# Up projections of the second-type MLPs as seven quarter products, with weight sums built in DRAM on the way there

## The chip, the cores and the metric

The kernel runs on one core of one Trainium2 chip. The metric is device microseconds of that core. The core has a matmul engine (TensorE, PE in the profile, with PEld for its weight loads), a vector engine (VectorE, DVE), an activation engine (ScalarE, ACT), a general engine (GpSimd, POOL) and SyncE (SP), which here only issues transfers. PSUM, where matmuls add up, has eight banks of 128 x 512 float32.

## The reference, cut to what matters

A sequence of 512 tokens with 1024 channels goes through one first-type block and then twice through a second-type layer. The change lies in the second half of that layer:

```python
for l in range(2):
    h = rmsnorm(x, g_mix[l])
    x = x + mixer(h)          # latent attention and a 31-tap convolution
    h2 = rmsnorm(x, g_ffn[l])
    z = dwconv3(h2 @ w_up[l]) + b_dw_ffn[l]   # w_up: 1024 x 5632, three taps over the tokens
    zg, zv = split(z)                          # 2816 gates, 2816 values
    x = x + (silu(zg) * zv) @ w_down[l]        # 2816 x 1024
return rmsnorm(x, g_final)
```

## The kernel before, in words

Channels lie on partitions and tokens along the free axis. Every product is made with float32 split in two: a high part (`xh`, `whi`, a cast) and a low part (`xl`, `wlo`, what the cast left). `mm3` issues three matmuls for one block of 128 x 128 weights: high by high (L380), high weight by low input (L381), low weight by high input (L382), each over 512 tokens.

Weights come as **units** of eight such blocks, in the order of use that `weight_plan` writes down. `prep` loads a unit on SP's queue into one of three `raw` buffers (512 KB), casts it on ACT to `whi` (L359) and subtracts on POOL to get `wlo` (L360); `whi` and `wlo` have four buffers each. `take` calls `prep` for up to three units ahead of the one in use, so these instructions stand in ACT's and POOL's queues among the rest. All five queues run in order.

The MLP of a second-type layer has 22 pairs of a gate and a value projection, each 128 columns wide. `norm_in` splits the eight tiles of `x` and adds up their squares in `acc`; the norm's factor `r` isn't needed by the matmuls and is multiplied in afterwards (`conv3`, L1289). The first two pairs run side by side, one k-step of all four projections after another (`proj_outer`), while the norm's last tiles are still being made; then comes the total of `acc` (a matmul with ones, `total`) and from it `r`. The other pairs run one projection after another, 8 blocks each. For each pair: `b` times `r` on DVE, ACT starts a convolution tile (`cg` or `cv`, L1292), DVE adds two taps (L1293, L1294), ACT makes the silu, DVE multiplies gate and value (L1308), ACT and DVE split the product (`ah`, `al`). After 11 pairs (`CHUNK2`) come eight down projections over these 11 tiles, added to `x` (L1313), then the other 11 pairs. The last two down projections of all run as two halves of 256 tokens (`proj_halves`), and the final norm follows.

Of the kernel before, what the change touches and what calls it, by code (L numbers as in the profile page):

```python
# [21 lines left out]
P = 128  # L22
S = 512
# [22 lines left out]
NF2 = FF2 // P  # L46
CHUNK2 = 11
GLU_EARLY = 3
# [28 lines left out]
def _span(c0, n=P):  # L77
    return np.arange(c0, c0 + n)


def weight_plan():
# [47 lines left out]
    for l in range(NL):  # L129
# [29 lines left out]
        for i in range(NYB, KT):  # L159
            add(tiles("w_o_2", l, k8, _span(P * i)))  # L160
        for c in range(NF2 // CHUNK2):
            fs = list(range(c * CHUNK2, (c + 1) * CHUNK2))
            if c == 0:
                add(outer("w_up_2", l, KT, [_span(P * f + o) for f in fs[:2] for o in (0, FF2)]))
                fs = fs[2:]
            for f in fs:
                add(tiles("w_up_2", l, k8, _span(P * f)))
                add(tiles("w_up_2", l, k8, _span(FF2 + P * f)))
            add([("w_down_2", l, P * k, _span(P * m)) for m in range(KT) for k in range(c * CHUNK2, (c + 1) * CHUNK2)])
    return units  # L170


def pack_weights(inputs, plan):
    out = np.zeros((len(plan), P, UNIT * P), np.float32)
    for u, blocks in enumerate(plan):
        for b, (name, l, r0, cols) in enumerate(blocks):
            w = inputs[name] if l is None else inputs[name][l]
# [4 lines left out]
    return out  # L182


# [69 lines left out]
class Kern:  # L254
    def __init__(self, tc, xT, w, vec, cst, pos, outT):
        self.tc, self.nc = tc, tc.nc
        self.xT, self.w, self.vec_d, self.cst_d, self.pos_d, self.outT = xT, w, vec, cst, pos, outT
        self.plan = weight_plan()
        self.units = {}
        self.prepped = 0  # L260
        self.cur, self.blk = 0, 0
        self.table, self.table_users = None, []


    def setup(self, ctx):
# [22 lines left out]
        self.epst = c.tile([P, 1], F32, name="epst")  # L288
        nc.gpsimd.memset(self.epst, EPS)
        self.lna = {}  # L290
        for n in (D, 512, QL, KVL):
# [58 lines left out]
    def prep(self, u, eng=None):  # L350
        nc = self.nc
        n = len(self.plan[u]) * P
        raw = self.wp.tile([P, UNIT * P], F32, name="raw", bufs=3)
        hi = self.wp.tile([P, UNIT * P], FR, name="whi")
        lo = self.wp.tile([P, UNIT * P], FR, name="wlo")
        cuts = (0, n) if eng is None else (0, n // 2, n)
        for cs in map(slice, cuts, cuts[1:]):
            nc.sync.dma_start(out=raw[:, cs], in_=self.w[u, :, cs])
            nc.scalar.copy(out=hi[:, cs], in_=raw[:, cs])  # L359
            (eng or nc.gpsimd).tensor_tensor(out=lo[:, cs], in0=raw[:, cs], in1=hi[:, cs].bitcast(F32), op=ALU.subtract)  # L360
        self.units[u] = (hi, lo)

    def take(self, n=1, ahead=AHEAD):
# [38 lines left out]
    def proj_outer(self, pool, tag, acts, n, parts=WHOLE, between=None):  # L402
# [90 lines left out]
    def norm_in(self, pool, gname, l, on_pool=KT - 2):  # L493
# [13 lines left out]

        def finish(pp, tag):
            r = self.rp.tile([P, S], F32, name="r", bufs=1)
            self.rsqrt(r, self.total(pp, tag, acc)[0], D)  # L510
            return r

# [469 lines left out]
    def layer2(self, l, carry=None):  # L982
# [301 lines left out]
        split_in()  # L1284
        ffc = tc.tile_pool(name="ffc", bufs=CHUNK2, reuse_waits="tile")
        fp = ffc.__enter__()

        def conv3(ps, f, tag):
            V.tensor_tensor(out=ps, in0=ps, in1=r, op=ALU.mult)  # L1289
            w3 = self.v("w_dw_ffn_2", l, 3 * f, 3)  # L1290
            c = fp.tile([P, S], F32, name=tag, bufs=2)
# [4 lines left out]

        for c in range(NF2 // CHUNK2):
            a = []
            pss = []
            if c == 0:  # L1300
                pss = self.proj_outer(pp, "b", acts, 4)
                r = fin(pp, "b")
            for f in range(c * CHUNK2, (c + 1) * CHUNK2):
                pg, pv = pss[2 * f : 2 * f + 2] if 2 * f < len(pss) else (self.proj(pp, "b", acts), self.proj(pp, "b", acts))
                cg = conv3(pg, f, "cg")
                cv = conv3(pv, NF2 + f, "cv")
                self.act(AF.Silu, out=cg, in_=cg)
                V.tensor_tensor(out=cg, in0=cg, in1=cv, op=ALU.mult)  # L1308
                a.append(self.split(fp, cg, ("ah", "al")))
            tail = 2 if l == NL - 1 and c == NF2 // CHUNK2 - 1 else 0  # L1310
            for m in range(KT - tail):
                ps = self.proj(pp, "b", a)
                V.tensor_tensor(out=self.x[m], in0=self.x[m], in1=ps, op=ALU.add)  # L1313
            if tail:
                self.final(pp, a)
        self._close(ffc)
        self._close(xg)
        self._close(pp_)

    def final(self, pp, a):  # L1320
# [16 lines left out]
        def half(j, ps, cs):  # L1337
            i = KT - 2 + j
            V.tensor_tensor(out=self.x[i][:, cs], in0=self.x[i][:, cs], in1=ps, op=ALU.add)
            gain(i, cs, cs.start == 0 or j == 0)  # L1340

        def norm(cs):
            self.rsqrt(r[:, cs], self.total(pp, "b", acc[:, cs], *late)[0], D)
            late.clear()
            for j in range(0, KT, OUT_TILES):
                o = op.tile([P, OUT_TILES, S // 2], F32, name="o")
                for i in range(OUT_TILES):
                    (G if j + i in OUT_POOL else V).tensor_tensor(out=o[:, i, :], in0=self.x[j + i][:, cs], in1=r[:, cs], op=ALU.mult)
                dst = self.outT[j * P : (j + OUT_TILES) * P, cs].rearrange("(i p) s -> p i s", p=P)
                (nc.sync if j // OUT_TILES % 2 else nc.scalar).dma_start(out=dst, in_=o)  # L1350
# [40 lines left out]
```

## Time and profile before

| | |
|---|---|
| median of 3 runs | 1880.58 us (1879.61 to 1883.46) |
| the profiled execution's own time | 1880.29 us |
| its span, first to last instruction | 1878.6 us |
| granted TensorE clock, mean | 0.998 |
| TensorE busy | 1839.2 us, 98% |
| DVE, ACT, POOL busy | 958.1, 946.3, 938.4 us |
| MLP of layer 0 and of layer 1 | about 924 to 1310 us and 1506 to 1867 us |

A row of the timeline gives start and duration in us, engine, line, operation and output<-input; where several alike follow each other it gives their count behind an x, and the time that they cover together. A row of the groups gives line, engine, operation, names and shapes, count, then busy us in all, mean ns of one, and the idle time ahead of them. A row of the windows gives the stretch, its length, then for PE, PEld, DVE, ACT and POOL busy us with the count of instructions, then the granted clock (1 is full speed), the share of the DMA engines that is busy, and GB/s. Matmuls overlap in the pipeline, so what one costs is read from start to start, not from its duration.

### The profile page before, as it was taken

How to read it: one execution, taken by the hardware profiler on the slowest of the kernel's cores; microseconds unless marked ns; L12 is line 12 of the kernel's file. 1: busy time of each engine (PE TensorE's matmuls, PEld its weight loads, DVE VectorE, ACT ScalarE, POOL GpSimd, SP SyncE). 2: the span in 40 equal slices, each digit the busy share in tenths (PEclk: the TensorE clock that was granted, in tenths of full speed). 3: DMA queues.
4: the chain of work that ended last, by engine and by line, in shares of the span. 5: the costliest groups of instructions: out<-in, count | busy, mean ns of one | idle time of the engine just before them, and what ended most of it. 6: DMA issues, size and time to landing. Idle time of an engine off the chain costs nothing.

```text
span 1878.6 us, 22097 instructions
## 1 busy us (share of the span) xinstructions
PE 1839.2 (98%) x8448; PEld 1495.8 (80%) x8448; DVE 958.1 (51%) x1420; ACT 946.3 (50%) x1442; POOL 938.4 (50%) x510
## 2 busy tenths in 40 slices
PE   8999999999999999999999999999999999999997
PEld 6877888888888888766888888888866788888886
DVE  4666552724022037997565225522898565405543
ACT  6766633643243347697554224433778554314442
POOL 5233444644444557866644444454966464444442
PEclk9999999999999999999999999999999999999999
DMA  5111223222222222200222222222210122222221
GB/s 188 68 57 62 79 101 135 93 94 101 92 99 98 94 90 71 98 29 21 94 106 95 97 101 91 101 101 90 91 51 23 64 99 101 101 91 101 100 91 56
DMA packets 48649, 164.89 MB, mean 88 GB/s; under 512 B 5536, under 2 KB 7584, under 8 KB 48544
## 3 DMA queue, kind: packets, MB, share of 16 engines
q1 hardware_dynamic: 46304, 160.34, 24.3%
q10 hardware_dynamic: 2240, 3.15, 0.5%
q8 instruction: 66, 1.08, 0.2%
q14 instruction: 39, 0.32, 0.1%
HBM read 161.37 MB, written 2.10 MB: 87 GB/s over the span
## 4 chain that ended last, share of the span: by engine, by line
PE 89%; DVE 6%; ACT 3%; issue 1%; POOL 1%; DMA 0%; SPq 0%; DVEq 0%; ACTq 0%; POOLq 0%
PE b L381 23%; PE b L382 23%; PE b L380 23%; PE mm L381 3%; PE s L1140 3%; PE mm L380 3%; PE mm L382 3%; PE t L1157 2%; DVE xl L452 1%; PE av L1162 1%; PE av L1163 1%; PE cv L480 1%; ACT whi L359 1%; DVE x L650 1%; PE b L480 1%
## 5 line engine op out<-in xcount | busy, mean ns | idle before, releaser
L360 POOL TENSOR_TENSOR wlo<-raw,whi 128x1024 fp32r<-128x1024 f32 x300 | 720.9, 2405 | 809.9 <-ACT whi L359 809.6
L359 ACT CAST whi<-raw 128x1024 fp32r<-128x1024 f32 (+1 forms) x302 | 313.6, 1040 | 506.4 <-PE b L381 414.6
L380 PE MATMUL b<-xh,whi 128*128 128x512 f32 (+1 forms) x1296 | 495.4, 382 | 2.7 <-ACT xh L451 2.7
L381 PE MATMUL b<-xl,whi 128*128 128x512 f32 (+1 forms) x1296 | 491.4, 379 | 3.4 <-DVE xl L452 3.4
L382 PE MATMUL b<-xh,wlo 128*128 128x512 f32 (+1 forms) x1296 | 491.1, 379 | 0.0
L381 PEld LDWEIGHTS b<-xl,whi 128*128 128x128 f32 x1296 | 244.1, 188 | 51.9 <-DVE xl L452 4.2
L380 PEld LDWEIGHTS b<-xh,whi 128*128 128x128 f32 x1296 | 244.2, 188 | 50.5 <-ACT xh L451 3.1
L382 PEld LDWEIGHTS b<-xh,wlo 128*128 128x128 f32 x1296 | 244.1, 188 | 45.6
L380 PE MATMUL b<-ah,whi 128*128 128x512 f32 (+1 forms) x646 | 243.6, 377 | 0.0
L381 PE MATMUL b<-al,whi 128*128 128x512 f32 (+1 forms) x646 | 243.2, 377 | 0.0
L382 PE MATMUL b<-ah,wlo 128*128 128x512 f32 (+1 forms) x646 | 243.2, 376 | 0.0
L381 PEld LDWEIGHTS b<-al,whi 128*128 128x128 f32 x646 | 121.6, 188 | 22.4
L380 PEld LDWEIGHTS b<-ah,whi 128*128 128x128 f32 x646 | 121.5, 188 | 22.4
L382 PEld LDWEIGHTS b<-ah,wlo 128*128 128x128 f32 x646 | 121.6, 188 | 22.0
L1228 POOL TENSOR_TENSOR cacc<-cacc,pd 128x510 f32<-128x510 f32 (+14 forms) x94 | 119.8, 1275 | 26.6 <-ACT pd L1226 22.8
L1212 DVE SCALAR_TENSOR_TENSOR cv<-u,vec,cv 128x497 f32<-128x497 f32 (+13 forms) x146 | 108.2, 741 | 8.4 <-ACT cv L1202 6.5
L1289 DVE TENSOR_TENSOR b<-b,r 128x512 f32<-128x512 f32 x88 | 61.0, 697 | 97.3 <-PE b L382 97.1
L1313 DVE TENSOR_TENSOR x<-x,b 128x512 f32<-128x512 f32 x30 | 20.6, 687 | 161.3 <-PE b L382 161.3
L448 ACT CAST ah<-cg 128x512 fp32r<-128x512 f32 x44 | 27.3, 621 | 98.7 <-DVE cg L1308 98.7
L380 PE MATMUL mm<-xh,whi 128*128 128x512 f32 x176 | 69.3, 394 | 0.0
L871 DVE TENSOR_TENSOR b<-rl,b 128x512 f32<-128x512 f32 x32 | 22.1, 696 | 92.5 <-ACT rl L870 92.5
L381 PE MATMUL mm<-xl,whi 128*128 128x512 f32 x176 | 68.7, 391 | 0.0
(430 smaller groups left out, 2851.0 us busy)
## 6 DMA issues: line engine op xcount, KB each, us to landing
raw<-w SPq DMA_DIRECT2D x295, 512.0 KB, 3.2
x<-xT SPq DMA_DIRECT2D x8, 256.0 KB, 6.5
x<-xT ACTq DMA_DIRECT2D x8, 256.0 KB, 4.8
raw<-w SPq DMA_DIRECT2D x7, 256.0 KB, 2.6
outT<-o ACTq DMA_DIRECT2D x4, 256.0 KB, 2.4
outT<-o SPq DMA_DIRECT2D x4, 256.0 KB, 2.5
vec<-vec SPq DMA_DIRECT2D x1, 363.0 KB, 6.9
f<-pos SPq DMA_DIRECT2D x1, 256.0 KB, 3.3
```

The source lines that it names most:

```text
L359: nc.scalar.copy(out=hi[:, cs], in_=raw[:, cs])
L360: (eng or nc.gpsimd).tensor_tensor(out=lo[:, cs], in0=raw[:, cs], in1=hi[:, cs].bitcast(F32), op=ALU.subtract)
L380: mm(ps, lhsT=wb[0], rhs=xb[0], start=start, stop=False, **kw)
L381: mm(ps, lhsT=wb[0], rhs=xb[1], start=False, stop=False, **kw)
L382: mm(ps, lhsT=wb[1], rhs=xb[0], start=False, stop=stop, **kw)
L448: nc.scalar.copy(out=hi, in_=src)
L480: self.nc.tensor.matmul(full[:, :n], lhsT=self.ones, rhs=a, start=i == 0, stop=i == len(parts) - 1)
L1140: mm(s, lhsT=q[:, qb * P : (qb + 1) * P], rhs=k, start=True, stop=True)
L1157: nc.tensor.transpose(pt[:, qb * P : (qb + 1) * P], probs[qb][:, t * P : (t + 1) * P], self.ident)
L1212: ins = V.scalar_tensor_tensor(out=acc[:, o], in0=us[i][:, u], scalar=self.v("w_dw_conv_2", l, i * CONV_K + k), in1=acc[:, o], op0=ALU.mul ...
L1228: G.tensor_tensor(out=acc[:, o], in0=acc[:, o], in1=pd, op=ALU.add)
L1289: V.tensor_tensor(out=ps, in0=ps, in1=r, op=ALU.mult)
```

## The change

In both layers pairs 0 to 3 stay as they were, and pairs 4 to 21 use a scheme of seven products (Strassen and Winograd's). A pair's weights are four quarters: `a11`, `a12` (gate, the first and the last four k-blocks), `a21`, `a22` (value). The inputs are four quarters too: k-blocks 0 to 3 or 4 to 7, tokens 0 to 255 or 256 to 511. Seven products of a weight quarter or sum (`S1` to `S4`) and an input quarter or sum (`B11`, `B21`, `T1` to `T4`, `B22`), with three copies (`snap`) and three additions (`plus`) between, give both projections. So a pair takes 7 x 4 x 3 = 84 matmuls of 256 columns in place of 2 x 8 x 3 = 48 of 512, and 28 blocks of weights in place of 16.

- **Input sums.** `quarter_inputs` multiplies `r` into `x` ahead of the products and makes the seven input matrices with their splits: per layer 27 instructions on DVE, 14 casts on ACT, 6 subtractions on POOL. The value comes out negated, which tap weights of the other sign (`wneg`, made at the start) take back; the multiplication by `r` falls away for these pairs. For that, `total` and `r` are made after three of the eight k-steps of `proj_outer` in place of after all.
- **Weight sums.** The quarters come in a new input `wq`. `S1` to `S4` of all pairs are built in DRAM while the kernel runs: 40 copies on ACT's queue and 40 adding transfers on POOL's queue, most of 1 MB (groups of four pairs) and some of 0.5 MB, each issued behind the cast or the subtraction of a unit in `SIDE`: every unit from 10 to 48, every second to 111, then every one, which reaches to about unit 121. Unit 29 to 48 is the end of block 1's mixer, 49 to 112 its MLP, 113 to 140 the mixer of layer 0.
- **Order.** Chunks are 7, 7 and 8 pairs in place of 11 and 11, so the additions to `x` are 24 per layer in place of 16. Each product pair's last two products come among the next pair's, at a chunk's end among the first three down projections. 355 units are loaded in place of 302; units of the new kind that hold parts of two matrices take two loads.
- **End.** Output tiles of the last four channel blocks of the left half are issued behind the right half's last addition to `x`.

```diff
-CHUNK2 = 11
+CHUNKS2 = (0, 7, 14, 22)
+PLAIN2 = 4
+OUTER2 = 2
+NDOWN = 3
+SUM_PAIRS = 4
+SIDE = {u: 1 for u in range(10, 140) if u < 49 or u > 112 or u % 2}
...
         self.units[u] = (hi, lo)
+        for _ in range(SIDE.get(u, 0)):
+            if self.side:
+                begin, on_pool = self.side.popleft()
+                self.issue_behind(begin(), rest if on_pool else cast)
...
+        def copy(dst, src):
+            return lambda: nc.scalar.dma_start(out=dst, in_=src)
+        def add(dst, src):
+            return lambda: nc.gpsimd.dma_start(out=dst, in_=src, accum_op=ALU.add, max_dma_last_dim=row)
...
             for k, a in enumerate(acts):
+                if k == OUTER_LAG + 2 and between is not None:
+                    between()
                 for ps in pss:
...
+        def norms():
+            rs.append(fin(pp, "b", True))
+            self.quarter_inputs(hp, ops, "g_ffn_2", l, rs[0][1])
+        pss = self.proj_outer(pp, "b", acts, 2 * OUTER2, between=norms)
+        pss += [self.proj(pp, "b", acts) for _ in range(2 * (PLAIN2 - OUTER2))]
...
+                    for ps in (pg, pv):
+                        V.tensor_tensor(out=ps, in0=ps, in1=r, op=ALU.mult)
+                    a.append(unit(f, pg, pv, self.v("w_dw_ffn_2", l, 3 * (NF2 + f), 3), False))
...
+                def p4(g):
+                    times(g["v"][:, L], "T4", False, True)
+                    plus(g["v"][:, R], g["g"][:, R], g["u3"])
+                def p3(g):
+                    times(g["g"][:, R], "B22", False, True)
+                    plus(g["g"][:, R], g["g"][:, R], g["u2"])
+                    a.append(unit(g["f"], g["g"], g["v"], self.wneg[l][:, 3 * g["f"] : 3 * g["f"] + 3]))
...
+                    times(g["v"][:, L], "B11", True, False)
+                    u1 = snap(g["v"][:, L])
+                    times(g["g"][:, L], "B21", True, True)
+                    plus(g["g"][:, L], g["g"][:, L], u1)
+                    if old is not None:
+                        p4(old)
+                    times(g["v"][:, L], "T2", False, False)
+                    g["u2"] = snap(g["v"][:, L])
+                    times(g["g"][:, R], "T1", False, False)
+                    if old is not None:
+                        p3(old)
+                    times(g["v"][:, L], "T3", False, False)
+                    g["u3"] = snap(g["v"][:, L])
+                    old = g
...
+        for k in range(0, KT // 2, 2):
...
+                    V.scalar_tensor_tensor(out=t[:, j], in0=self.x[k0 + j], scalar=self.v(gname, l, k0 + j), in1=r, op0=ALU.mult, op1=ALU.mult)
...
+            def put(name, src, eng):
+                hi, lo = (t[:, k : k + 2] for t in ops[name])
+                A.copy(out=hi, in_=src)
+                eng.tensor_tensor(out=lo, in0=src, in1=hi.bitcast(F32), op=ALU.subtract)
...
+            put("B11", b11, G)
+            put("B21", b21, G)
+            t1 = temp()
+            V.tensor_tensor(out=t1, in0=b11, in1=b12, op=ALU.subtract)
...
+            put("T2", t2, V)
+            put("T1", t1, V)
...
+                    if behind is not None and j >= KT // 2 and not on_pool:
+                        self.issue_behind(ins, behind)
```

**How the order moves.** DVE, behind the norm's factor of layer 0, in the kernel before: `b_7868` to `b_7871` are the four projections of pairs 0 and 1 (gate, value, gate, value), and the convolution of pair 0 follows three multiplications by `r`.

```order
L491 SCALAR_TENSOR_TENSOR r_7992<-b_7993,r_7992 128x512 [waits DVE_49]
L1289 TENSOR_TENSOR b_7868<-b_7868,r_7992 128x512 [waits DVE_49,PE_49]
L1289 TENSOR_TENSOR b_7869<-b_7869,r_7992 128x512 [waits PE_49]
L1289 TENSOR_TENSOR b_7870<-b_7870,r_7992 128x512 [waits PE_49]
L1293 SCALAR_TENSOR_TENSOR cg_8002<-b_7868,vec_67,cg_8002 128x511 [waits Activation_49]
L1293 SCALAR_TENSOR_TENSOR cv_8007<-b_7869,vec_67,cv_8007 128x511 [waits Activation_49]
L1294 SCALAR_TENSOR_TENSOR cg_8002<-b_7868,vec_67,cg_8002 128x511 [waits DVE_49]
L1294 SCALAR_TENSOR_TENSOR cv_8007<-b_7869,vec_67,cv_8007 128x511 [waits DVE_49]
L1293 SCALAR_TENSOR_TENSOR cg_8019<-b_7870,vec_67,cg_8019 128x511 [waits Activation_49]
L1308 TENSOR_TENSOR cg_8002<-cg_8002,cv_8007 128x512 [waits DVE_49,Activation_49]
```

DVE at the same place in the changed kernel: `b_8011` to `b_8014` are pairs 0 and 1, `b_8199` to `b_8294` the four plain projections behind them, `T4l` the last input sum.

```order
L1448 TENSOR_TENSOR b_8014<-b_8014,r_8063 128x512 [waits PE_49]
L1540 TENSOR_TENSOR T4l_8005<-t_8112,T4h_8004 128x512 [waits Activation_49]
L1448 TENSOR_TENSOR b_8199<-b_8199,r_8063 128x512 [waits PE_49]
L1448 TENSOR_TENSOR b_8230<-b_8230,r_8063 128x512 [waits PE_49]
L1448 TENSOR_TENSOR b_8262<-b_8262,r_8063 128x512 [waits PE_49]
L1448 TENSOR_TENSOR b_8294<-b_8294,r_8063 128x512 [waits PE_49]
L1425 SCALAR_TENSOR_TENSOR cg_8335<-b_8011,vec_67,cg_8335 128x511 [waits Activation_49]
L1425 SCALAR_TENSOR_TENSOR cv_8339<-b_8012,vec_67,cv_8339 128x511 [waits Activation_49]
L1426 SCALAR_TENSOR_TENSOR cg_8335<-b_8011,vec_67,cg_8335 128x511 [waits DVE_49]
L1426 SCALAR_TENSOR_TENSOR cv_8339<-b_8012,vec_67,cv_8339 128x511 [waits DVE_49]
L1425 SCALAR_TENSOR_TENSOR cg_8352<-b_8013,vec_67,cg_8352 128x511 [waits Activation_49]
L1435 TENSOR_TENSOR cg_8335<-cg_8335,cv_8339 128x512 [waits DVE_49,Activation_49]
```

All eight multiplications now stand ahead of the first convolution step, the last of them behind the end of the last plain projection.

ACT in the changed kernel, the same stretch: `whi_8401` is the fourth unit of the first products, in the buffer that the last plain projection used.

```order
L406 CAST whi_8296<-raw_8295 128x1024 [waits DMAHW6_49,DMAHW7_49,PE_49,Pool_49]
L406 CAST whi_8401<-raw_8400 128x1024 [waits DMAHW0_49,DMAHW1_49,PE_49,Pool_49]
L1424 ACTIVATE cg_8335<-b_8011,vec_67 128x512
L1424 ACTIVATE cv_8339<-b_8012,vec_67 128x512
L1424 ACTIVATE cg_8352<-b_8013,vec_67 128x512 [waits DVE_49,PE_49]
L1424 ACTIVATE cv_8356<-b_8014,vec_67 128x512 [waits DVE_49]
L385 ACTIVATE cg_8335<-cg_8335 128x512 [waits DVE_49,Activation_49]
L561 CAST ah_8346<-cg_8335 128x512 [waits DVE_49]
L1424 ACTIVATE cv_8372<-b_8230,vec_67 128x512 [waits Activation_49]
L1454 COPY snap_8419<-b_8398 128x256 [waits PE_49]
```

The first convolution step `cg_8335` stands behind that cast, and the first `snap` behind silu and split of pair 0.

TensorE in the changed kernel, from the last plain projection to the first product: `b_8398` is the accumulator of the first product, in the bank of `b_8011`.

```order
L493 MATMUL b_8294<-xh_7949,wlo_8202 128x512
L491 MATMUL b_8294<-xh_7951,whi_8201 128x512
L492 MATMUL b_8294<-xl_7952,whi_8201 128x512
L493 MATMUL b_8294<-xh_7951,wlo_8202 128x512
L491 MATMUL b_8398<-B11h_7994,whi_8232 128x256 [waits DVE_49,Activation_49]
L492 MATMUL b_8398<-B11l_7995,whi_8232 128x256
```

The first product waits for DVE's last reading of pair 0's gate, the second tap `cg_8335<-b_8011` (L1426).

POOL in the changed kernel, block 1: the first adding transfers (512 rows of 2 KB) among the subtractions.

```order
L452 DMA S1_0_0_138<-wq 512x512 [waits DMAHW1_49]
L407 TENSOR_TENSOR wlo_1411<-raw_1409,whi_1410 128x1024 [waits DMAHW2_49,PE_49,Activation_49]
L407 TENSOR_TENSOR wlo_1525<-raw_1523,whi_1524 128x1024 [waits DMAHW4_49,PE_49,Activation_49]
L452 DMA S1_0_1_142<-wq 512x512
L407 TENSOR_TENSOR wlo_1565<-raw_1563,whi_1564 128x1024 [waits DMAHW5_49,PE_49,Activation_49]
...
L452 DMA S1_0_2_146<-wq 512x512
```

POOL had the subtractions alone there; an adding transfer now stands behind every second unit.

## Rows read from the trace of the kernel before

**Rows 1.** Page, part 1: busy time of TensorE.

```profile
PE 1839.2 (98%) x8448; PEld 1495.8 (80%) x8448; DVE 958.1 (51%) x1420; ACT 946.3 (50%) x1442; POOL 938.4 (50%) x510
```

**Rows 2.** Windows, MLP of layer 0 and of layer 1: busy time per engine.

```profile
945.00:1100.00 155.00, 155.00 (x683) 127.97 (x683) 70.34 (x98) 61.65 (x76) 67.37 (x29) 1.00 0.28 98
...
1527.00:1700.00 173.00, 173.00 (x763) 142.86 (x763) 75.09 (x105) 66.79 (x82) 76.23 (x32) 1.00 0.28 97
```

**Rows 3.** Timeline of TensorE, start of layer 0's MLP: start, duration.

```profile
923.73 0.39 PE L380 MATMUL b<-xh,whi 128*128 128x512 f32 x1
923.96 0.39 PE L381 MATMUL b<-xl,whi 128*128 128x512 f32 x1
```

**Rows 4.** Timeline of TensorE in the last down projections, 256 columns.

```profile
1862.04 0.28 PE L381 MATMUL b<-al,whi 128*128 128x256 f32 x1
1862.16 0.28 PE L382 MATMUL b<-ah,wlo 128*128 128x256 f32 x1
```

**Rows 5.** Timeline of the weight loads beside them.

```profile
1862.05 0.19 PEld L382 LDWEIGHTS b<-ah,wlo 128*128 128x128 f32 x1
```

**Rows 6.** Groups by line and shape, 945 to 1100 us (POOL, ACT, DVE).

```profile
L360 POOL TENSOR_TENSOR wlo<-raw,whi 128x1024 fp32r<-128x1024 f32 x29 | 69.6, 2401 | 89.1 <-ACT whi L359 89.1
...
L359 ACT CAST whi<-raw 128x1024 fp32r<-128x1024 f32 x29 | 30.5, 1052 | 58.1 <-PE b L381 58.0
L1292 ACT ACTIVATE cg<-b,vec 128x512 f32<-128x512 f32 x11 | 8.5, 772 | 3.3 <-DVE b L1289 3.3
...
L344 ACT ACTIVATE cg<-cg 128x512 f32<-128x512 f32 x11 | 6.9, 631 | 12.2 <-DVE cg L1294 12.2
L448 ACT CAST ah<-cg 128x512 fp32r<-128x512 f32 x11 | 6.8, 621 | 23.1 <-DVE cg L1308 23.1
...
L1289 DVE TENSOR_TENSOR b<-b,r 128x512 f32<-128x512 f32 x22 | 15.1, 695 | 16.7 <-PE b L382 16.6
...
L1294 DVE SCALAR_TENSOR_TENSOR cg<-b,vec,cg 128x511 f32<-128x511 f32 x11 | 8.2, 746 | 0.2
```

**Rows 7.** Page, part 6: weight loads, time from issue to landing.

```profile
raw<-w SPq DMA_DIRECT2D x295, 512.0 KB, 3.2
```

**Rows 8.** Groups by line and shape, whole span: 128x256 steps of DVE and ACT.

```profile
L534 DVE TENSOR_TENSOR x<-x,b 128x256 f32<-128x256 f32 x32 | 13.3, 416 | 0.7
...
L462 ACT ACTIVATE sq<-x 128x256 f32<-128x256 f32 x31 | 12.6, 407 | 8.9 <-DVE x L1339 6.6 <-POOL acc L463 2.0
```

**Rows 9.** Timeline of DVE and POOL, norm ahead of layer 0's MLP.

```profile
919.43 9.67 DVE L452 SCALAR_TENSOR_TENSOR xl<-x,vec,xh 128x512 fp32r<-128x512 f32 x5
...
932.00 0.68 DVE L463 TENSOR_TENSOR acc<-acc,sq 128x512 f32<-128x512 f32 x1
...
920.60 2.86 POOL L360 TENSOR_TENSOR wlo<-raw,whi 128x1024 fp32r<-128x1024 f32 x1
```

**Rows 10.** Timeline of DVE, the norm's factor of layer 0's MLP made.

```profile
949.50 0.69 DVE L491 SCALAR_TENSOR_TENSOR r<-b,r 128x512 f32<-128x512 f32 x1
```

**Rows 11.** Timeline of DVE and POOL, first pair of layer 1.

```profile
1537.38 1.73 DVE L1308 TENSOR_TENSOR cg<-cg,cv 128x512 f32<-128x512 f32 x1
...
1536.16 2.41 POOL L360 TENSOR_TENSOR wlo<-raw,whi 128x1024 fp32r<-128x1024 f32 x1 [5.12 <-ACT whi L359]
```

**Rows 12.** Timeline and windows of TensorE, end of block 1: idle, then clock.

```profile
696.03 0.38 PE L380 MATMUL b<-xh,whi 128*128 128x256 f32 x1 [2.32 <-ACT xh L451]
697.45 0.39 PE L381 MATMUL b<-xl,whi 128*128 128x256 f32 x1 [1.03 <-DVE xl L452]
...
699.00:703.00 4.00, 4.00 (x21) 3.64 (x20) 3.90 (x11) 2.72 (x7) 2.40 (x3) 0.62 0.18 68
```

**Rows 13.** DMA rate in 40 slices, and ACT's issues, 290 to 330 us.

```profile
GB/s 0 279 246 0 213 311 123 348 270 279 373 408 268 45 33 274 217 0 0 139 373 12 0 106 377 41 0 0 4 266 254 0 0 0 164 356 4 0 0 29
...
296.20 3.09 ACTq L314 DMA_DIRECT2D x<-xT  x6
```

**Rows 14.** Waits of TensorE from 1864 us to the end.

```profile
PE b L480 <- DVE acc L463: 0.5, 1, 0.5
```

More of the change, by code (lines that the diff above doesn't have):

```diff
@@ L78, in _span, with chunks2 @@
     return np.arange(c0, c0 + n)
+def chunks2():
+    return [range(a, b) for a, b in zip(CHUNKS2, CHUNKS2[1:])]
 def weight_plan():
@@ L160, in weight_plan @@
             add(tiles("w_o_2", l, k8, _span(P * i)))
[L161 to L169, printed above, removed]
+        ffn = [("w_up_2", l, P * k, _span(P * f + o)) for k in range(KT) for f in range(OUTER2) for o in (0, FF2)]
+        ffn += [("w_up_2", l, P * k, _span(P * f + o)) for f in range(OUTER2, PLAIN2) for o in (0, FF2) for k in range(KT)]
+        for ks in chunks2():
+            quarter = lambda which, f: [(which, l, f, kk) for kk in range(KT // 2)]
+            before = None
+            for f in ks:
+                if f >= PLAIN2:
+                    ffn += quarter("a11", f) + quarter("a12", f)
+                    if before is not None:
+                        ffn += quarter("a22", before)
+                    ffn += quarter("S2", f) + quarter("S1", f)
+                    if before is not None:
+                        ffn += quarter("S4", before)
+                    ffn += quarter("S3", f)
+                    before = f
+            down = [("w_down_2", l, P * k, _span(P * m)) for k in ks for m in range(NDOWN)]
+            ffn += down[:4] + quarter("a22", before) + down[4:8] + quarter("S4", before) + down[8:]
+            ffn += [("w_down_2", l, P * k, _span(P * m)) for m in range(NDOWN, KT) for k in ks]
+        add(ffn)
     return units
@@ L289, in setup @@
         nc.gpsimd.memset(self.epst, EPS)
+        self.wneg = {}
+        for l in range(NL):
+            t = c.tile([P, 3 * NF2], F32, name=f"wneg{l}")
+            nc.gpsimd.tensor_scalar(out=t, in0=self.v("w_dw_ffn_2", l, 3 * NF2, 3 * NF2), scalar1=-1.0, scalar2=None, op0=ALU.mult)
+            self.wneg[l] = t
         self.lna = {}
@@ L355, in prep @@
         lo = self.wp.tile([P, UNIT * P], FR, name="wlo")
[L356 to L360, printed above, removed]
-        self.units[u] = (hi, lo)
+        if eng is None and any(b[0] in QUARTERS + SUMS for b in self.plan[u]):
+            for c0, c1, src in self.sources(u):
+                nc.sync.dma_start(out=raw[:, c0:c1], in_=src)
+            cuts = ((0, n),)
+        else:
+            cuts = ((0, n),) if eng is None else ((0, n // 2), (n // 2, n))
+            for c0, c1 in cuts:
+                nc.sync.dma_start(out=raw[:, c0:c1], in_=self.w[u, :, c0:c1])
@@ L1295, in conv3, with unit @@
             return c
[L1297 to L1315, printed above, removed]
+        def unit(f, pg, pv, wv, in_psum=True):
+            cg = conv3(pg, self.v("w_dw_ffn_2", l, 3 * f, 3), f, "cg")
+            cv = conv3(pv, wv, NF2 + f, "cv")
+            to = pg if in_psum else cg
+            self.act(AF.Silu, out=to, in_=cg)
+            V.tensor_tensor(out=to, in0=to, in1=cv, op=ALU.mult)
+            return self.split(fp, to, ("ah", "al"))
```

173 lines of the change are left out of this document (160 added, 13 removed).

## The prediction

> **What bounds the kernel now.** I read the busy times first. TensorE is busy for 1839.2 of 1878.6 us [rows 1]; the profiled execution took 1880.29 us, 1.7 us more than its span, and lies 0.3 us under the median, so I work from 1880.3 us. The windows then tell whether that holds where the change is made: in both layers' MLPs TensorE is busy for the whole stretch at full clock, while DVE, ACT and POOL are at 39% to 45% and the DMA engines at 28% [rows 2]. There the time is the number of matmuls by their spacing, and only what changes these two, or makes TensorE wait, can move the end. All other engines have room before, so the question is whether they still have it after.
>
> **The change part by part: matmuls.** The spacing is read from start to start: 0.227 us for 512 columns, from 923.73 to 923.96 [rows 3] (24 matmuls of a unit take 5.44 us), and 0.120 us for 256 columns [rows 4]. A plain pair takes 48 x 0.2267 = 10.88 us, a product pair 84 x 0.120 = 10.08 us. One pair saves 0.80 us, 36 pairs 28.9 us. The eighth fewer multiplications would be 1.36 us a pair, 49 us in all, if 256 columns took half of 512; 13 ns more for each short matmul takes 20 us of that.
>
> Each of those short matmuls had a weight load of its own, and these follow each other in 0.12 us too although one lasts 0.19 us [rows 5], so the loads overlap with the matmuls and I take 0.120. The Trainium skill speaks against that: TensorE: Matmul & The Clock Gate, "The mechanism", lets a weight load overlap with matmuls in flight only if it goes to another group of rows of the array, and its section on LDWEIGHTS gives 107 ns for 128 columns. With its 109 and 216 ns for matmuls a pair would then go from 48 x 0.323 = 15.5 to 84 x 0.216 = 18.1 us, some 94 us slower in all, near 1997 us with the waits below. The trace has neither spacing.
>
> **Start of each MLP.** Taken per layer, with layer 0 as the example.
>
> The total now stands after three k-steps. The outer product starts at 923.73 [rows 3]; 36 matmuls are through at 931.9. DVE's last addition to `acc` starts at 932.00 and takes 0.68 us [rows 9], so TensorE waits until 932.7 and a little for the signal: 0.9 us. Before, the total came 13 us later and waited for nothing.
>
> The first product waits for a PSUM bank: that of pair 0's gate, until DVE has read it for the second tap. In DVE's order that step stands behind the multiplication of the last plain projection, and in ACT's order the convolution stands behind a cast that waits for the same projection's end. From that end the chain is cast 1.05, `cg` 0.77, first tap of the gate 0.75, first tap of the value 0.75, second tap of the gate 0.75 [rows 6], 4.1 us in all. Before, pair 0's steps ran while TensorE did the next pairs and waited for nothing [rows 2]. Above this floor, `quarter_inputs` may still be in DVE's way: 27 instructions that cost 0.7 us alone (19 us), 16 of them with two SBUF inputs. Such ones took 1.93 us each beside POOL's subtractions and additions (5 in 9.67 us, [rows 9]) and 1.73 us once beside a `wlo` [rows 11]. `r` was done 4.7 us behind the outer product's end, at 950.2 [rows 10], and will be at about 938 now; TensorE gets to the first product at 969 (192 matmuls of 512 from 923.73, the wait of 0.9, as much for the total). In these 31 us eight multiplications of 0.70 us [rows 6] are due too, so at 1.0 us each DVE's work is 27 + 5.6 = 33 us, a little late. A walk through the queues with stretched durations gives 5.4 us of wait, which I take, between 4.1 and 8.
>
> The first `snap` stands on ACT behind pair 0's silu and split. From the bank's release: second tap of the value 0.75, first tap of pair 1's gate 0.75, product of gate and value 0.7 to 1.7, `ah` 0.62, a `cv` 0.77, `snap` 0.41 [rows 6, 8, 11], 4.0 to 5.0 us; TensorE has two products of 1.44 us to do meanwhile and waits 1.1 to 2.1 for the third. I take 1.8, and 1.7 more for the rest: four plain pairs leave DVE some 17 us of taps and splits that run into the first product pairs, whose `plus` steps release products. Together 3.5 us, between 1.1 and 6.
>
> A wait of that length can cost clock. At the end of block 1 came waits of 2.3 and 1.0 us with one matmul between, and the clock from 699 to 703 was 0.62 of full speed [rows 12], that is 1.5 us lost. Part of such a loss lies under other waits: 1.2 us, between 0 and 1.7.
>
> Sum per layer 0.9 + 5.4 + 3.5 + 1.2 = 11.0 us, for two 22 us (bounds 12 and 33).
>
> **Steady product pairs.** A pair of 10.08 us needs 3.5 units, one in 2.88 us, where a unit lasted 5.44 us. POOL: 3.5 x 2.40 = 8.4 us. ACT: 3.5 x 1.05, three `snap` of 0.41, two starts of 0.77, silu 0.63, `ah` 0.62: 7.7 us. DVE: three `plus` of 0.42, four taps of 0.75, two of 0.7: 5.7 us [rows 6, 8]. Transfers: 1.84 MB, 182 GB/s, while the slices show up to 408 GB/s [rows 13]. None is over 85%. A `raw` buffer's round is issue 0.4, landing 2.85, cast 1.05, subtraction 2.4 [rows 6, 7], with queueing some 7.2 us for three buffers: 2.4 us a unit, 0.5 under the need. I cost it at nothing; without that cover see below. The two products that close a chunk leave 6.8 us for a chain of about 6 us (`plus`, tap steps, silu, product, split) before the last block of `down` needs them: 0 to 1 us, six times; I take 1 us.
>
> **Weight sums.** 75 MB are written under block 1 and the start of layer 0's mixer. The DMA engines are at 28% there as elsewhere, and a load's landing (3.2 us, [rows 7]) is far under the distance to its use of more than 5.4 us a unit. An issue on ACT's queue costs 0.5 us (six in 3.09, [rows 13]), 40 of them beside casts of 1.05 us that have a unit's 5.44 us. No row shows what an adding transfer costs POOL: nothing at best, and 2.6 us at 1 MB by 408 GB/s if POOL is held for all of it; with a `wlo` that makes 5.0 of the 5.44 us of a unit. I take 0, between 0 and 5 us. By the Trainium skill, DMA: Bandwidth & Descriptors, such a transfer takes 2.0 us and its bytes by 436 GB/s, 4.4 us here by estimate, and no run here shows it.
>
> **End.** The right half's total waits 0.5 us for `acc` [rows 14], behind output multiplications that now come later: 0.5 us gained.
>
> Sum: 1880.3 - 28.9 + 22 + 1 + 0 - 0.5 = 1874 us. With all bounds low 1863, all high 1896.
>
> **Rivals.**
> - **The start is covered.** If DVE gets to the convolution at the floor of 4.1 us, the products behind don't wait and the clock holds, a layer costs 0.9 + 4.1 = 5.0 us: 1880.3 - 28.9 + 10 - 0.5 = 1861 us. For it: DVE is at 45% [rows 2], the two-input steps are 0.7 us when alone. Against it: the queues are in order and the rows of the order put `snap` behind pair 0.
> - **Weights come too late (slower).** POOL at 83% and ACT at 76% both work on each unit in turn, and `wlo` took up to 2.86 us beside DVE [rows 9]. The two MLPs use 126 units in product pairs. From 2.94 us a unit on (0.06 x 126 = 7 us) the gain that I forecast is gone. A round of the three buffers of 9 us, which is 1.8 us of queueing over the 7.2, makes 3.0 us a unit, 15 us lost: 1889 us. Against it: four buffers of `whi` and `wlo` even out single delays, and only an average counts.
> - **Adding transfers hold POOL.** In the mixers POOL has convolution work too and a transfer can't hide there as in an MLP. Five of them at 2.6 us bare make 13 us: 1887 us.
> - **The short matmuls don't gain.** At 10.88 / 84 = 0.1295 us a matmul the products save nothing, and the start's waits stay: 1903 us. Against it [rows 4, 5]. The rule on weight loads would go far beyond; the trace leaves it next to no chance.
>
> **How the numbers follow.** 0.45 for the forecast (its own range 1868 to 1880), 0.27 for a covered start (1852 to 1867), 0.15 for late weights (1882 to 1900), 0.08 for POOL held, 0.05 for matmuls without gain. About 0.2%, 3.8 us, is what a measurement tells from no change. Faster than 1876.8: 0.30 of the first, all of the second, 0.03 of the others, 0.60. Within: 0.14 of the first, 0.04 of the others, 0.18. Slower: 0.22. The range 1857 to 1889 leaves out a quarter of the covered start, half of the late weights and the last case, under 0.2.
>
> **What would show it.** In the profile after: 256-column matmuls 0.120 us apart in the product pairs, 10.1 us a pair, or TensorE's waits there name `whi` or `wlo` (late weights); the first product of a layer waiting 4 to 8 us, released by DVE's second tap, and then `snap`; a granted clock under 1 behind it; no new waits of TensorE before about 924 us, or POOL late behind adding transfers. The prediction is wrong if the waits at the starts are over 33 us or under 12 in all, or if the steady pairs are off 10.1 us by more than 0.3.

## The result, and the profile after

The changed kernel takes 1896.09 us (median of 6 runs, 1889.06 to 1900.9), the kernel before 1881.01 us (1879.61 to 1883.46): 1.0078 times the time before, 95% interval 1.0057 to 1.0099. It is slower by 15 us; 1874 us was forecast, and the range ended at 1889. The profiled execution is the slowest of the six: 1900.9 us, with a span of 1899.2 us and a mean clock of 0.986.

The busy time of TensorE in the changed kernel:

```profile
PE 1835.5 (97%) x9726; PEld 1539.6 (81%) x9726; DVE 1019.6 (54%) x1520; ACT 1044.9 (55%) x1634; POOL 1127.0 (59%) x618
```

TensorE is busy 4 us less than before [rows 1] while the span is 20 us longer, so waits were added. Its waits by what ended them (us in total, times, longest):

```profile
PE b L491 <- DVE cg L1426: 7.7, 2, 3.8
PE zC L778 <- DVE x L769: 6.0, 6, 2.1
...
PE zA L778 <- DVE x L769: 4.2, 3, 2.0
...
PE b L593 <- DVE acc L1177: 3.7, 1, 3.7
...
PE zB L778 <- DVE x L769: 3.6, 3, 1.6
...
PE b L593 <- DVE acc L576: 0.8, 2, 0.4
```

Only the first and the last row lie in the MLPs. The `z` rows are block 1's stick-breaking attention (L778; `x` at L769 is the low part of its logarithms), L1177 is the norm at the end of block 1. The first matmul of layer 0's MLP, at 923.73 us before [rows 3], comes at 959.22 us:

```profile
959.22 0.40 PE L491 MATMUL b<-xh,whi 128*128 128x512 f32 x1
```

It is 35.5 us late before the first new product. From there the changed kernel gains: layer 0's MLP takes 359.9 us before and 350.1 us after from the outer product to the next mixer's first matmul, layer 1's 363.4 and 353.9 us to the last matmul of all. The mixer between them takes 4.4 us longer.

The clock falls where TensorE waits, in the attention and at the first products (windows, columns as in [rows 2]):

```profile
76.00:88.00 12.00, 9.15 (x33) 7.38 (x33) 5.12 (x7) 5.45 (x10) 2.35 (x1) 0.72 0.39 132
148.00:164.00 16.00, 12.75 (x47) 10.25 (x48) 8.38 (x10) 6.74 (x13) 3.87 (x3) 0.79 0.78 197
...
1008.00:1012.00 4.00, 3.68 (x17) 3.71 (x18) 4.00 (x8) 2.58 (x6) 0.00 (x0) 0.50 0.40 134
```

At the start of layer 0's products the chain runs as it was foretold, in the timeline of ACT and DVE:

```profile
1004.34 1.04 ACT L406 CAST whi<-raw 128x1024 fp32r<-128x1024 f32 x1 [2.94 <-PE b L492]
1005.29 0.77 ACT L1424 ACTIVATE cg<-b,vec 128x512 f32<-128x512 f32 x1
...
1006.09 0.75 DVE L1425 SCALAR_TENSOR_TENSOR cg<-b,vec,cg 128x511 f32<-128x511 f32 x1 [0.88 <-ACT cg L1424]
1006.76 0.75 DVE L1425 SCALAR_TENSOR_TENSOR cv<-b,vec,cv 128x511 f32<-128x511 f32 x1
1007.43 0.74 DVE L1426 SCALAR_TENSOR_TENSOR cg<-b,vec,cg 128x511 f32<-128x511 f32 x1
...
1011.32 0.36 ACT L1454 COPY snap<-b 128x256 f32<-128x256 f32 x1
```

The cast that waited for the last plain projection, `cg`, two first taps and the second tap of the gate end at 1008.2 us, and the first product starts at 1008.3 after 3.8 us. The `snap` behind is done at 1011.7; TensorE doesn't wait for it, since from 1008 to 1012 us the clock is at 0.50, the 1.2 GHz level, and the two products ahead take 5.2 us, to 1013.57, where their 24 matmuls take 2.8 us in the steady pairs below.

In the steady pairs nothing waits. Window of product pairs in the changed kernel:

```profile
1115.00:1145.00 30.00, 30.00 (x258) 30.00 (x257) 16.71 (x28) 20.95 (x33) 26.01 (x12) 1.00 0.55 184
```

The window counts 258 matmuls, with those that its ends cut. From start to start they are 0.118 us apart, 9.9 us a pair, a little better than the 0.120 of [rows 4]. POOL is at 87%, and weights are never late.

### The profile page after: what moved, and what is told of

Read it like the earlier page. It is cut to its first block, busy times and chain, and to the rows that moved or that the text cites. A ratio compares the mean times of both kernels' runs of the same rounds, so it can differ in the third digit from the quotient of the medians.

```text
span 1899.2 us, 25711 instructions
## 1 busy us (share of the span) xinstructions
PE 1835.5 (97%) x9726; PEld 1539.6 (81%) x9726; DVE 1019.6 (54%) x1520; ACT 1044.9 (55%) x1634; POOL 1127.0 (59%) x618
## 4 chain that ended last, share of the span: by engine, by line
PE 84%; DVE 9%; ACT 3%; issue 1%; POOL 1%; DMA 1%; ACTq 0%; DVEq 0%; SPq 0%; POOLq 0%
PE b L491 21%; PE b L492 21%; PE b L493 21%; PE s L1259 3%; PE mm L492 3%; PE mm L491 3%; PE mm L493 3%; DVE xl L565 2%; PE t L1276 2%; DVE x L769 1%; ACT whi L406 1%; PE av L1281 1%; PE av L1282 1%; PE cv L593 1%; PE b L593 1%
## 5 line engine op out<-in xcount | busy, mean ns | idle before, releaser
L407 POOL TENSOR_TENSOR wlo<-raw,whi 128x1024 fp32r<-128x1024 f32 (+1 forms) x354 | 854.1, 2416 | 630.0 <-ACT whi L406 619.8
L406 ACT CAST whi<-raw 128x1024 fp32r<-128x1024 f32 (+1 forms) x356 | 370.0, 1041 | 490.7 <-PE b L492 353.2
L491 PE MATMUL b<-xh,whi 128*128 128x512 f32 (+1 forms) x720 | 274.7, 382 | 2.7 <-ACT xh L564 2.7
L492 PE MATMUL b<-xl,whi 128*128 128x512 f32 (+1 forms) x720 | 270.5, 376 | 4.0 <-DVE xl L565 3.9
L493 PE MATMUL b<-xh,wlo 128*128 128x512 f32 (+1 forms) x720 | 269.7, 375 | 0.0
L492 PEld LDWEIGHTS b<-xl,whi 128*128 128x128 f32 x720 | 136.2, 189 | 33.1 <-DVE xl L565 5.0
L491 PEld LDWEIGHTS b<-xh,whi 128*128 128x128 f32 x720 | 136.5, 190 | 31.2 <-ACT xh L564 3.1
L493 PEld LDWEIGHTS b<-xh,wlo 128*128 128x128 f32 x720 | 136.2, 189 | 26.1
L1459 DVE TENSOR_TENSOR b<-b,snap 128x256 f32<-128x256 f32 x108 | 46.4, 429 | 85.0 <-PE b L493 84.9
L493 PE MATMUL mm<-xh,wlo 128*128 128x512 f32 x176 | 71.5, 406 | 0.0
## 6 DMA issues: line engine op xcount, KB each, us to landing
S<-wq POOLq DMA_DIRECT2D x32, 1024.0 KB, 13.7
```

Source lines behind the costliest of these rows:

```text
L406: cast = nc.scalar.copy(out=hi[:, cs], in_=raw[:, cs])
L407: rest = (eng or nc.gpsimd).tensor_tensor(out=lo[:, cs], in0=raw[:, cs], in1=hi[:, cs].bitcast(F32), op=ALU.subtract)
L491: mm(ps, lhsT=wb[0], rhs=xb[0], start=start, stop=False, **kw)
L492: mm(ps, lhsT=wb[0], rhs=xb[1], start=False, stop=False, **kw)
L493: mm(ps, lhsT=wb[1], rhs=xb[0], start=False, stop=stop, **kw)
L1459: V.tensor_tensor(out=out, in0=a, in1=b, op=ALU.add)
```

## What the transfers cost

**Left out** (run e1). The loads of sums read quarters of the new input.

```diff
-SIDE = {u: 1 for u in range(10, 140) if u < 49 or u > 112 or u % 2}
+SIDE = {}
...
-                reg, i = divmod(f - PLAIN2, SUM_PAIRS)
-                src = self.sum_of[l, name, reg]...
+                src = self.wq[l, SUMS.index(name), f - PLAIN2]
```

> The 80 transfers are left out, and the loads of the sums S1 to S4 read quarters of the new input in their place, so the weights of those products are not the sums; all else is as in the changed kernel. Up to the first product of layer 0 the order on TensorE, VectorE and ScalarE is then that of the kernel before. Theory: the transfers cost all of what the trace shows ahead of layer 0's MLP (35 us late), and the products themselves gain 9 us in each MLP, so about 1862 us (1858 to 1866). Rival: the products or their input sums disturb the mixers by themselves (other memory, other order), then over 1880 us.

1867.30 us (1866.95 to 1867.83), 0.9931 [0.9918, 0.9943] of the kernel before. Without the transfers the kernel is 28.8 us faster than the changed one and 13 us faster than the kernel before. It was 5 us over what the theory gave: not all of the 35.5 us ahead of layer 0's MLP are the transfers' (see the place of the tiles). Up to there DVE and ACT run all their instructions in the order of the kernel before; in the changed kernel 22 of 709 on DVE and 20 of 812 on ACT stand elsewhere.

**Alone** (run e3): the kernel before with `wq`, `sums` and the issue in `prep`, and nothing else.

```diff
         self.units[u] = (hi, lo)
+        for _ in range(SIDE.get(u, 0)):
+            if self.side:
+                begin, on_pool = self.side.popleft()
+                self.issue_behind(begin(), rest if on_pool else cast)
```

> The kernel before with only the 80 transfers added, at the same units; the sums are built and not used. Theory: it loses what the changed kernel loses ahead of layer 0's MLP, 30 to 36 us: 1911 to 1917 us. Rival: the transfers cost little by themselves, then within 5 us of 1881 us.

1907.53 us, 1.0143 [1.0129, 1.0157]: 27.4 us, with nearly the same waits at the same places as the changed kernel, and with its order on DVE and ACT up to layer 0's MLP. The cost belongs to the transfers and not to the products.

**Made small** (run e4).

```diff
-            return lambda: nc.scalar.dma_start(out=dst, in_=src)
+            return lambda: nc.scalar.dma_start(out=dst[:16, :64], in_=src[:16, :64])
...
-            return lambda: nc.gpsimd.dma_start(out=dst, in_=src, accum_op=ALU.add, max_dma_last_dim=row)
+            return lambda: nc.gpsimd.dma_start(out=dst[:16, :64], in_=src[:16, :64], accum_op=ALU.add, max_dma_last_dim=row)
```

> The changed kernel with each of the 80 transfers cut to 16 rows of 64 numbers (4 KB), issued at the same places; the loads of sums read quarters of the new input, so the sums are not used. If the traffic of the transfers is what costs, as the theory has it where waits for loads grow, the time falls to that without transfers, about 1862 us. Rival: their places in the queues of ScalarE and GpSimd and the order that comes with them cost, then 1885 to 1897 us.

1868.26 us, 0.9935 [0.9921, 0.9948]: within 1 us of none at all. The 80 issues in ACT's and POOL's queues cost next to nothing. It looks like traffic, but the run doesn't separate that: the order that the scheduler chooses depends on the size of the transfers, and with small ones ACT and DVE get nearly the order of the kernel before (4 and 2 instructions stand elsewhere). The waits of TensorE in the attention are those of before too:

```profile
PE zC L777 <- DVE x L768: 2.7, 4, 1.2
PE zB L777 <- DVE x L768: 2.6, 2, 1.6
```

**Where the order bites.** In the changed kernel ACT waits longer in the attention for a buffer of `whi` that TensorE still reads, and DVE's low parts (L769) take longer. Before, ACT's waits and DVE's group in the attention (us in total, times, longest; then count, busy us, mean ns):

```profile
ACT whi L359 <- PE mm L381: 4.3, 5, 2.3
...
L650 DVE TENSOR_TENSOR x<-x 128x512 fp32r<-128x512 f32 (+1 forms) x24 | 21.9, 913 | 10.3 <-ACT x L649 10.0
```

After:

```profile
ACT whi L406 <- PE mm L492: 12.9, 6, 4.9
...
ACT whi L406 <- PE mm L493: 4.2, 1, 4.2
...
L769 DVE TENSOR_TENSOR x<-x 128x512 fp32r<-128x512 f32 (+1 forms) x24 | 28.6, 1190 | 11.2 <-ACT x L768 10.9
```

One such place in the timeline of the changed kernel, on ACT, DVE, POOL and TensorE:

```profile
156.51 1.05 ACT L406 CAST whi<-raw 128x1024 fp32r<-128x1024 f32 x1 [4.20 <-PE mm L493]
...
157.46 0.61 ACT L768 CAST x<-x 128x512 fp32r<-128x512 f32 x1
...
158.11 2.43 DVE L769 TENSOR_TENSOR x<-x 128x512 fp32r<-128x512 f32 x1 [0.99 <-ACT x L768]
...
157.65 2.34 POOL L407 TENSOR_TENSOR wlo<-raw,whi 128x1024 fp32r<-128x1024 f32 x1 [8.12 <-ACT whi L406]
...
160.59 0.80 PE L778 MATMUL zA<-x,ntri 128*128 128x512 f32 x1 [1.97 <-DVE x L769]
```

The weight cast `whi` stands ahead of the attention's cast (L768), waits 4.2 us for TensorE to free its buffer, and the attention's cast waits behind it. Then POOL starts `wlo` 0.46 us before DVE gets to its subtraction, which has two inputs in SBUF: it lasts 2.43 us, and TensorE waits 1.97 us more. Alone it takes 0.69 us, as in the kernel before:

```profile
116.27 0.69 DVE L650 TENSOR_TENSOR x<-x 128x512 fp32r<-128x512 f32 x1 [0.69 <-ACT x L649]
```

The Trainium skill, SBUF — State Buffer, "Who interferes with whom", has VectorE with two SBUF inputs and a GpSimd instruction that reads SBUF contend for one port pair, and the second blocked until the first is through. The two rows agree: DVE's subtraction ends 0.55 us behind POOL's, a little less than it takes alone.

**Large transfers in the good order** (run e6). The instructions on DVE, ACT and POOL are numbered as they are made, and each is tied behind the one that precedes it in the order of the kernel with small transfers, up to layer 0's MLP; the transfers are at full size and used.

```diff
+                j = len(self._log)
+                self._log.append(ins)
+                for a, b in NEIGHBOURS.get(j, ()):
+                    self._tc.add_manual_dep(self._log[b].ins, self._log[a].ins.name, QUEUE, reason="queue order")
```

> The changed kernel, all 80 transfers at full size, with VectorE's, ScalarE's and GpSimd's instructions up to layer 0's MLP held in the order that they have in the kernel with small transfers (1868.3 us). If the order that the scheduler chose with the large transfers in its reckoning costs (weight casts ahead of the attention's casts on ScalarE, where they wait for a free buffer), it falls to about 1868 to 1875 us. If the traffic itself costs (loads that land later, GpSimd held by the adding transfers), it stays at 1890 to 1897 us.

1874.76 us (1872.19 to 1877.14), 0.9971 [0.9959, 0.9982]. The order is worth 21.3 us, and the attention's waits are those of before again:

```profile
PE zC L817 <- DVE x L305: 2.7, 4, 1.2
PE zB L817 <- DVE x L305: 2.6, 2, 1.6
```

The 6.5 us over the run with small transfers are not all traffic. In the traces 1.7 us of them lie ahead of layer 0's MLP, which starts at 935.4 us here and at 933.7 us there; the last transfer is issued at 745 us. Another 4.5 us lie behind, in the middle chunk of product pairs: between the down projections on either side it takes 74.9 us here and 72.6 us there, in both layers. Run e5 (below), with all transfers at full size, has the 72.6 us, so the transfers don't cause that. Windows in this chunk of layer 0, in this run, with small transfers, and in run e5:

```profile
1070.00:1110.00 40.00, 40.00 (x342) 40.00 (x341) 21.97 (x36) 27.66 (x42) 33.32 (x15) 1.00 0.62 188
...
1070.00:1110.00 40.00, 40.00 (x355) 40.00 (x354) 23.19 (x38) 28.92 (x46) 34.65 (x15) 1.00 0.60 186
...
1090.00:1130.00 40.00, 40.00 (x356) 40.00 (x355) 22.66 (x37) 28.17 (x43) 35.09 (x16) 1.00 0.62 189
```

From start to start the matmuls are 0.118, 0.113 and 0.113 us apart. What sets that stays open; some 2 us are left for the traffic and for POOL, which the transfers hold for 41 us in all here and for 33 us when small.

**ACT's order alone** (run e14): the same with the list for ACT only.

> The changed kernel with ScalarE's order alone held, VectorE and GpSimd left to the scheduler. If it is the weight casts that stand ahead of the attention's casts on ScalarE, nearly all of the 21 us come back: 1875 to 1880 us. If VectorE's order is as much of it, 1883 us or more.

1879.67 us, 0.9996 [0.9987, 1.0005]: 16.4 of the 21.3 us come from ACT's queue, inside the first theory's range. DVE's order stays nearly that of the changed kernel (9 of 709 instructions stand elsewhere). TensorE's waits in the attention:

```profile
PE zB L817 <- DVE x L305: 3.2, 3, 1.6
PE zC L817 <- DVE x L305: 2.7, 5, 1.2
PE zC L817 <- ACT x L305: 1.7, 3, 1.3
```

**Moved away from the attention** (run e2).

```diff
-SIDE = {u: 1 for u in range(10, 140) if u < 49 or u > 112 or u % 2}
+SIDE = {u: 1 for u in range(29, 140)}
```

> The changed kernel with the 80 transfers behind every unit from 29 on, so they end at about unit 109, in block 1's MLP, and none lies in the stick-breaking attention or in layer 0's mixer. Under the theory of the order and under that of the traffic the 22 us lost in the attention come back, and most of the 6 us in layer 0's mixer: 1868 to 1876 us. If the transfers cost wherever they stand, since a unit of the MLP now carries 1.5 MB in 5.4 us, over 1885 us.

1877.77 us, 0.9985 [0.9976, 0.9994]: 18.3 us better than the change, 2 us short of the range that was expected.

## Where the tiles lie

In the changed kernel block 1's matmuls on the split `x` are slower. Nothing there was changed; but the two tables `wneg` of 264 bytes a partition, padded to 288, move all later tiles by 576 bytes. Run e10 moves them so in the kernel before, with every engine's order the same:

```diff
         nc.gpsimd.memset(self.epst, EPS)
+        shift = c.tile([P, 144], F32, name="shift")
+        nc.gpsimd.memset(shift[:, :1], 0.0)
```

> The kernel before with 576 bytes a partition of constants that nothing reads, so that all later tiles lie where they lie in the changed kernel; the order on all engines is the same. If the place of the tiles is what slows the matmuls on the split x, it is 4 to 9 us slower than the kernel before: 1884 to 1890 us. If not, 1880 us.

1892.14 us, 1.0065 [1.0052, 1.0078]: 576 bytes that nobody uses cost 12 us, 3 us more than expected. Layer 0's MLP starts at 932.52 us, 8.8 us late, and at 932.58 us in run e1. Before, 80 us in block 1's second run of up projections:

```profile
520.00:600.00 80.00, 80.00 (x354) 66.24 (x353) 22.90 (x33) 30.26 (x43) 34.25 (x15) 1.00 0.27 98
```

With the shift:

```profile
525.00:605.00 80.00, 80.00 (x344) 64.46 (x343) 22.00 (x32) 29.85 (x42) 33.62 (x14) 1.00 0.29 93
```

354 and 344 matmuls: 0.227 and 0.233 us from start to start. Run e7 gives the tables 512 bytes each in the changed kernel.

```diff
-            t = c.tile([P, 3 * NF2], F32, name=f"wneg{l}")
+            t = c.tile([P, P], F32, name=f"wneg{l}")[:, : 3 * NF2]
```

> The changed kernel with the two small tables of negated tap weights given 512 bytes a partition each in place of 264, and no other difference: all later tiles lie 1024 bytes further than in the kernel before in place of 576. In the changed kernel the matmuls of 512 columns that read the split x are 0.235 us apart in block 1's MLP where they were 0.228. If that comes from where the tiles lie, they go back to 0.228 and the time falls by 4 to 9 us, to about 1889 us. If it comes from other work, 1896 us as before.

1892.73 us, 1.0066 [1.0052, 1.0080], 3.4 us better, a little under the range. The windows, in block 1 as above, and in steady product pairs:

```profile
540.00:620.00 80.00, 80.00 (x355) 66.24 (x354) 21.52 (x32) 31.91 (x45) 39.02 (x19) 1.00 0.68 190
...
1085.00:1115.00 30.00, 30.00 (x252) 30.00 (x251) 16.46 (x27) 21.17 (x32) 24.77 (x12) 1.00 0.58 184
```

The matmuls of 512 columns are back at 0.227 us, and those of 256 columns go from 0.118 to 0.120 us, 10.08 us a pair. The 576 bytes slow the first and speed the second. That is why the products alone give the same time at either place: run e1 starts layer 0's MLP 9.9 us behind the next run, and is 9.1 us faster from there.

**Products alone, at the place of e7** (run e13): run e1 with the edit of e7.

> The kernel without transfers (the loads of sums read quarters, so the weights of those products are not the sums) with the small tables at 512 bytes a partition, so that neither the transfers nor the place of the tiles weigh on what comes ahead of layer 0's MLP. What is left is the products alone against the kernel before. With product pairs of 10.08 us, as the trace with these tables has them, and a start that costs 5 to 6 us a layer (bank wait 3.8, clock some 1.5, total 0.4): 1880.2 - 28.9 + 12 - 0.5, about 1863 us. Had the start cost the 22 us that the prediction took, 1873 us.

1867.67 us, 0.9932 [0.9920, 0.9945]; 12.4 us gained, 4.7 fewer than expected. TensorE's waits in layer 0's MLP:

```profile
PE b L490 <- DVE cg L1425: 3.8, 1, 3.8
PE b L592 <- DVE acc L575: 0.7, 1, 0.7
```

## The start, and the best version

**Convolution tiles of their own** (run e5). `cg` and `cv` lay in memory that the plain projections' inputs held to the end.

```diff
-        hp_ = tc.tile_pool(name="hp", bufs=1, reuse_waits="tile")
+        hp_ = tc.tile_pool(name="hp", bufs=1, side="right", reuse_waits="tile")
...
+        cgc = tc.tile_pool(name="cgc", bufs=2, side="right", reuse_waits="tile")
+        cp = cgc.__enter__()
...
-            c = fp.tile([P, S], F32, name=tag, bufs=2)
+            c = cp.tile([P, S], F32, name=tag, bufs=2)
```

> The changed kernel with the convolution tiles of the MLP in memory of their own (where the input sums were made) in place of memory that the plain projections' inputs hold until the last plain projection is through. Theory: the wait of 3.8 us ahead of the first product of each layer comes from that; it falls under 1 us, the clock stays up behind it (some 1.7 us), and the two layers gain 8 to 11 us: about 1886 us. Rival: the first product then waits for the cast or subtraction of its weights or for the first copy of a product just as long, then 1893 us or more.

1899.92 us, no better than the change. The first product no longer waits, but the third does, for `snap`, 5.8 us in place of 3.8. TensorE's wait, and ACT's timeline in front of it:

```profile
PE b L491 <- ACT snap L1456: 11.5, 2, 5.8
```

```profile
1005.45 1.98 ACT L406 CAST whi<-raw 128x1024 fp32r<-128x1024 f32 x2
1007.33 1.14 ACT L561 CAST ah<-cg 128x512 fp32r<-128x512 f32 x2
1008.37 0.37 ACT L1456 COPY snap<-b 128x256 f32<-128x256 f32 x1
```

DVE had been busy without a break with input sums, stretched beside POOL; pair 0's product came late, and on ACT two weight casts and two splits then stand ahead of `snap`. So the rival held: with the memory freed, the next thing in the queues makes TensorE wait, and longer.

**Order and place together** (run e11): e6 with the edit of e7.

> All transfers at full size, the order of the kernel with small transfers up to layer 0's MLP, and the tables at 512 bytes. If the order and the place of the tiles are two costs that add up, the order takes 21 us off the changed kernel's 1896 and the place 4 to 9 more: 1863 to 1871 us. If the place only counted where the order was good or bad, 1874 us.

1870.45 us (1869.61 to 1872.18), 0.9951 [0.9937, 0.9964]: the two add up, 4.3 us for the place, and this is the fastest kernel that computes the whole reference, 2.8 us over the products alone.

**And the transfers from unit 29 on** (run e12).

> The same, with the transfers behind every unit from 29 on. If some 6 us of traffic are left in the attention and in layer 0's mixer (what the run with the held order has over that with small transfers), 2 to 6 us under the run before this one: 1860 to 1866 us. If the traffic costs as much in the MLP of block 1, the same as that.

1874.03 us, 0.9964 [0.9952, 0.9977], a miss: 3.6 us slower than from unit 10. In the norm ahead of block 1's MLP, in the timeline of DVE and POOL, and TensorE's waits there:

```profile
358.74 7.53 DVE L305 SCALAR_TENSOR_TENSOR xl<-x,vec,xh 128x256 fp32r<-128x256 f32 x2
...
358.56 1.01 POOL L305 DMA_DIRECT2D S<-wq  x1
359.23 1.10 POOL L305 TENSOR_TENSOR acc<-acc,sq 128x256 f32<-128x256 f32 x1
359.93 2.69 POOL L305 TENSOR_TENSOR wlo<-raw,whi 128x1024 fp32r<-128x1024 f32 x1
362.23 1.06 POOL L305 TENSOR_TENSOR acc<-acc,sq 128x256 f32<-128x256 f32 x1
362.91 2.67 POOL L305 TENSOR_TENSOR wlo<-raw,whi 128x1024 fp32r<-128x1024 f32 x1
...
PE b L531 <- DVE xl L305: 6.1, 1, 6.1
```

Two low parts on DVE take 7.53 us beside POOL's queue, which by now holds the issue of an adding transfer, two additions of squares and two `wlo` with hardly a gap. In run e11, with the transfers from unit 10, the two take 3.53 us and TensorE waits 0.6; without transfers they take 0.62 and 2.32 us in run e13, and it waits 0.9.

## Why the prediction was wrong

**The step that failed** is "Weight sums", taken at 0, between 0 and 5 us; the kernel with them takes 28.8 us longer than without. What it weighed was right: the issues cost at most 1 us (e4), loads land hardly later (3.5 us, 3.2 before), and an adding transfer holds POOL for 0.9 to 1.8 us. It lands 13.7 us after its issue, not the 4.4 that the prediction worked out. Landing and issue in the changed kernel:

```profile
raw<-w SPq DMA_DIRECT2D x215, 512.0 KB, 3.5
...
S<-wq POOLq DMA_DIRECT2D x32, 1024.0 KB, 13.7
...
148.28 1.25 POOL L452 DMA_DIRECT2D S<-wq  x1
```

What it left out is that 1 MB transfers change the order in which a scheduler puts other instructions. I looked at the order where the products start and not where the transfers stand, in the attention, a chain in which each step on ACT or DVE is waited for. 21.3 us are that order (e6), 1 us the issues, and some 2 us the traffic and the holding of POOL; 4.5 us are the middle chunks' slower matmuls, which run e5 doesn't have although it has the transfers.

**The rivals** had POOL held (13 us) and late weights (15 us); neither happened: in e6 POOL is held by the adding transfers as long as in the changed kernel, 41 us in all. The clock fell only behind waits; but six of its falls are ahead of layer 0's MLP, where the kernel before has one.

**The matmuls** were right: 10.08 us a pair at the place of e7, 9.9 in the changed kernel; the weight loads hide, against the rule that was weighed. One number of the working is wrong: half of 0.2267 us is 0.1133, so a short matmul costs 7 ns more than half a long one, not 13; the 20 us that follow are right for 7. That the place of tiles moves long and short matmuls by 2 to 3% was in none of the terms.

**The start** was mis-sized: 11.0 us a layer taken, and layer 0 of e13 (352.7 us against 359.9) gains 7.2 of the 14.4 us of its 18 pairs, so it costs 7.2. In layer 0 the total waits 0.7 (0.9 taken), the bank 3.8 (5.4; the floor was 4.1), the first pairs nothing (3.5), the clock 1.7 (0.86 over the 12 us from 972 us; 1.2 taken), and 1 us I can't place. Layer 1 (357.9 us against 363.4) costs 8.9: its clock is 0.72 over the 12 us from 1546 us, 3.4 us lost in place of 1.7. So the two starts cost 16 us where 22 were taken. The products alone give 1867.7 where my sum said 1874; the range would have held that.

**Open:** by what rule the place of two operands sets the spacing of matmuls, and why in e1, e4 and e5 pairs of the middle chunk took 9.5 us and of the last chunk 9.9, where the changed kernel has 9.9 in both. No run tells it apart.

## What to carry to other kernels

Transfers that are off every path can still cost through a scheduler whose order depends on their size: compare the order of the engines at each place where such transfers stand, above all in a chain of small steps, and hold the order there if it moved. Where an in-order queue serves both a chain and a supply, an instruction of the supply that waits for a buffer stops the chain, and what it releases on GpSimd may then block VectorE as well. A few hundred bytes of new constants can move the time by as much as a change gains (12 us each here): compare at the same place, or pad.

## What the runs showed of the hardware that I had not expected

- A shift of all later tiles by 576 bytes a partition took matmuls of 512 columns on the split `x` from 0.227 to 0.233 us. With a shift of 1024 bytes they were at 0.227, and the products' matmuls of 256 columns at 0.120 us, where 576 bytes had them at 0.118 and, in one chunk of some runs, at 0.113.
- 80 transfers of 4 KB on ACT's and POOL's queues cost 1 us in all. At 0.5 to 1 MB, in a held order of the other instructions, they cost 2.8 us in all (e11 against e13).
- An adding transfer of 1 MB took 13.7 us from issue to landing, a plain load of 0.5 MB 3.5 us.
